# Column pairs of a split-precision decoder trunk: longer low weight parts, whole-row buffers, high-part products first

## The chip, the cores and the metric

The kernel runs on one core of one Trainium2 chip. The metric is device time in microseconds of one execution. Verdicts compare timed runs of two kernels on the same chip; the profile is one further execution, taken by the hardware profiler, and it has a time of its own.

## The reference

A trunk of two layers on 256 tokens of width 2048: a retention layer (8 heads, keys of 256, values of 512) with a squared-ReLU MLP, then a latent-attention layer (16 heads) with another such MLP. All inputs are float32.

```python
def sq_relu_mlp(h, w1, w2):
    return jnp.square(jax.nn.relu(h @ w1)) @ w2        # 2048 -> 8192 -> 2048

for layer in range(DEPTH):                              # DEPTH = 2
    if layer < N_A_LAYERS:
        h = rms_norm(x, norm_mix[layer])
        x = x + retention(h, ret_w_in[layer], ret_w_out[layer], ret_cos, ret_sin)
    else:
        ...
        h = rms_norm(x, norm_mix[layer])
        x = x + mla_attention(h, mla_w_dq[j], ..., mla_w_o[j], k_nope, k_pe, v, mla_cos, mla_sin)
    x = x + sq_relu_mlp(rms_norm(x, norm_mlp[layer]), mlp_w1[layer], mlp_w2[layer])
```

Nearly all of the work is in matrix products of the 256 tokens with weights that are read once from memory.

## The kernel before

**Two parts per number.** TensorE multiplies in the type fp32r. To keep float32 accuracy each operand is split in two: ScalarE rounds the value to fp32r (the high part, a copy, L188) and VectorE subtracts that from the value (the low part, L189). A product of two blocks is then three matmuls into one PSUM bank: activation high by weight high (L364), activation high by weight low (L365), activation low by weight high (L366). The activations are the stationary operand, 128 by 128, and the weights the moving one, 128 rows by 512 columns.

**Quads and pairs.** Most weights are laid out on the host in quads (`_quads`, L1110): 256 rows by 1024 columns, four blocks of 128 by 512, one load of 1 MB into a tile of 2048 columns. `gemm_pair` (L341) computes 1024 output columns (a column pair) as a loop over the quads of these columns, eight for 2048 rows, and adds into PSUM. A quad is multiplied with the 2 by 2 blocks of the activations (two groups of 128 tokens, two blocks of 128 rows) in one of two ways, chosen per quad by the tuple `kinds`: with eight products of blocks, or with seven, a scheme of the Strassen family. For seven, the quad needs sums of weight blocks: VectorE makes four of them in three instructions (L323, L327, L328: 1024, 512 and 512 columns) in two tiles `u` of 1024 columns, and the sums are split into parts as the blocks are. After the last quad `pair_out` (L376) copies the banks to SBUF (ScalarE) and combines them (VectorE).

**Parts of a quad.** `parts` (L302) splits up to 1024 columns at once into one buffer `wh` and one `wl` of 1024 columns each; there are five of either tag. A quad of eight makes two such pairs of parts; a quad of seven makes four: blocks b11 and b22, block b21 alone (512 columns), the sums u2 and u4, the sums u1 and u3. The products that use them are issued right after each, product by product.

**Other users of the same buffers.** `stream` (L210) feeds the plain products (`gemm`, `gemm_t`, `gemm_blocks`): it loads a chunk of up to 2048 columns and splits it in two halves, each into a `wh` and a `wl` of its own. Raw loads of either kind share three buffers (`raw`), and all are issued by SyncE's queue.

**What runs between quads.** Every quad and every chunk ends in a `tick`, which runs the functions that have become due: the evacuation of a finished pair, transposes of results into new activations, the chain of attention for a head. The order on each engine is then set by a scheduler, which moves instructions against each other where dependences allow; each engine executes its queue in that order, and an instruction that waits holds those behind it. `queued_behind` (L284) ties the low parts of blocks behind the last of the sums (`summed_up`, L328).

The stages in order are: retention (query and key products by `gemm_t`, gate and value products by pairs, output products by pairs), the first MLP (pairs `u` and `d`), the products of the latent attention (`kd`, `dqp`, `dq`, `ku`, `uq`, `wo`, `wop`), the second MLP. `kinds` comes from tuples at the top of the file: (1, 3, 5, 7), (3, 5, 7) and (5, 7) in the MLPs, (2, 4, 6, 7) and (5, 7) in retention, (3, 4, 6, 7) and (3, 5, 6, 7) in attention; the quads named have seven products.

## Time and profile before

| | |
|---|---|
| three timed runs | 2484.82, 2486.37, 2487.07 us |
| median | 2486.37 us |
| profiled execution | 2490.05 us |
| its span, first to last instruction | 2488.3 us |
| mean granted TensorE clock of it | 0.997 of full speed |
| read from memory | 479.14 MB |
| written | 39.85 MB |

The profile lists instructions by engine: PE is TensorE's matmuls, PEld its weight loads, DVE VectorE, ACT ScalarE, POOL GpSimd, SP SyncE. A group of instructions is named by its source line, its engine and its tiles, as out<-in; the numbers behind it are busy time, mean length, and the idle time of the engine just before it with what ended that. Names begin with the stage: `rp` gate and value pairs of retention, `ro` its output pairs, `u` and `d` the two products of an MLP. The end of a matmul is modelled, and matmuls overlap, so that spacing from start to start is the measure of TensorE's pace.

### The profile page before, as it was taken

To read this page: it belongs to the slowest core of one execution; us is meant where nothing else is said; L and a number is where in the kernel's file an instruction comes from. 1 tells how busy PE (TensorE), PEld (TensorE's weight loads), DVE (VectorE), ACT (ScalarE), POOL (GpSimd) and SP (SyncE) were. 2 spreads that over 40 slices of the span, in tenths; PEclk is the share of its full clock that TensorE was granted. 3 is DMA by queue.
4 is the path that set the end of the run, shared out by engine and by line. 5 is a ranking of instruction groups with operands and counts; after the bars stand their busy time and mean duration, and the time that the engine had idled before them with its cause. 6 is when DMAs were issued, how large, how long until landed. Compare 5 with 4: busy or idle time off the path is not lost.

```text
span 2488.3 us, 31679 instructions
## 1 busy us (share of the span) xinstructions
PE 2457.3 (99%) x11614; PEld 2066.6 (83%) x11614; DVE 2198.9 (88%) x2892; ACT 1648.2 (66%) x2297; POOL 251.4 (10%) x308
## 2 busy tenths in 40 slices
PE   9999999999999999999999999999999999999999
PEld 7788888888888888878888888998888888888887
DVE  6799999889899989989999988776899999999996
ACT  6566666566676767667676777666776667676663
POOL 7300001000010010010110101110000100100100
PEclk9999999999999999999999999999999999999999
DMA  9555558556565686685785554444555866857864
GB/s 312 190 190 204 177 193 256 207 174 223 200 216 191 207 252 200 213 260 187 238 269 203 192 206 174 155 146 170 174 207 207 236 224 200 260 202 223 260 212 167
DMA packets 93403, 521.04 MB, mean 209 GB/s; under 512 B 11072, under 2 KB 12224, under 8 KB 40000
## 3 DMA queue, kind: packets, MB, share of 16 engines
q1 hardware_dynamic: 71856, 472.83, 54.4%
q0 software_dynamic: 21248, 46.15, 8.8%
q8 instruction: 91, 1.49, 0.2%
q14 instruction: 64, 0.52, 0.1%
q10 hardware_dynamic: 144, 0.05, 0.0%
HBM read 479.14 MB, written 39.85 MB: 209 GB/s over the span
## 4 chain that ended last, share of the span: by engine, by line
PE 86%; DVE 7%; DMA 3%; ACT 2%; issue 1%; POOL 1%; DVEq 0%; ACTq 0%; POOLq 0%
PE u_c L365 6%; PE u_c L366 6%; PE u_c L364 6%; PE d_c L365 6%; PE d_c L366 6%; PE d_c L364 6%; PE rq_acc L276 2%; PE rp_c L364 2%; PE rp_c L365 2%; PE rp_c L366 2%; PE rk_acc L276 2%; PE u_p L364 2%; PE u_p L365 2%; PE u_p L366 2%; PE d_p L364 2%; PE d_p L366 2%
## 5 line engine op out<-in xcount | busy, mean ns | idle before, releaser
L189 DVE TENSOR_TENSOR d_wl<-d_raw,d_wh 128x1024 fp32r<-128x1024 f32 (+1 forms) x256 | 279.0, 1115 | 27.0 <-ACT d_wh L188 26.9
L188 ACT CAST d_wh<-d_raw 128x1024 fp32r<-128x1024 f32 (+1 forms) x256 | 241.9, 975 | 81.9 <-PE d_c L366 47.9
L189 DVE TENSOR_TENSOR u_wl<-u_raw,u_wh 128x1024 fp32r<-128x1024 f32 (+1 forms) x256 | 277.6, 1111 | 16.2 <-ACT u_wh L188 16.1
L188 ACT CAST u_wh<-u_raw 128x1024 fp32r<-128x1024 f32 (+1 forms) x256 | 240.9, 972 | 65.3 <-PE u_c L366 47.0
L365 PE MATMUL u_c<-u_wl,n 128*128 128x512 f32 x712 | 277.9, 390 | 2.8 <-DVE u_wl L189 2.8
L364 PE MATMUL u_c<-u_wh,n 128*128 128x512 f32 x712 | 278.4, 392 | 0.0
L366 PE MATMUL u_c<-u_wh,n 128*128 128x512 f32 x712 | 277.2, 389 | 0.0
L365 PE MATMUL d_c<-d_wl,hid 128*128 128x512 f32 x660 | 257.2, 390 | 3.0 <-DVE d_wl L189 3.0
L364 PE MATMUL d_c<-d_wh,hid 128*128 128x512 f32 x660 | 258.5, 392 | 0.0
L366 PE MATMUL d_c<-d_wh,hid 128*128 128x512 f32 x660 | 257.0, 389 | 0.0
L188 ACT CAST u_wh<-u_u 128x1024 fp32r<-128x1024 f32 x104 | 107.7, 1054 | 110.1 <-DVE u_u L328 55.7
L188 ACT CAST d_wh<-d_u 128x1024 fp32r<-128x1024 f32 x100 | 103.8, 1055 | 99.2 <-DVE d_u L328 55.1
L365 PEld LDWEIGHTS u_c<-u_wl,n 128*128 128x128 f32 x712 | 133.8, 188 | 32.3 <-DVE u_wl L189 5.2
L366 PEld LDWEIGHTS u_c<-u_wh,n 128*128 128x128 f32 x712 | 133.7, 188 | 27.7
L364 PEld LDWEIGHTS u_c<-u_wh,n 128*128 128x128 f32 x712 | 133.7, 188 | 27.2
L188 ACT CAST rp_wh<-rp_raw 128x1024 fp32r<-128x1024 f32 x112 | 104.1, 945 | 70.6 <-PE rp_c L366 42.3
L365 PEld LDWEIGHTS d_c<-d_wl,hid 128*128 128x128 f32 x660 | 124.0, 188 | 29.5 <-DVE d_wl L189 4.4
L366 PEld LDWEIGHTS d_c<-d_wh,hid 128*128 128x128 f32 x660 | 123.9, 188 | 25.8
L364 PEld LDWEIGHTS d_c<-d_wh,hid 128*128 128x128 f32 x660 | 124.0, 188 | 25.0
L189 DVE TENSOR_TENSOR u_wl<-u_u,u_wh 128x1024 fp32r<-128x1024 f32 x104 | 123.8, 1220 | 4.5 <-ACT u_wh L188 4.3
L189 DVE TENSOR_TENSOR rp_wl<-rp_raw,rp_wh 128x1024 fp32r<-128x1024 f32 x112 | 118.8, 1089 | 5.3 <-ACT rp_wh L188 5.0
L189 DVE TENSOR_TENSOR d_wl<-d_u,d_wh 128x1024 fp32r<-128x1024 f32 x100 | 118.8, 1219 | 2.6 <-ACT d_wh L188 2.6
(567 smaller groups left out, 6607.6 us busy)
## 6 DMA issues: line engine op xcount, KB each, us to landing
u_raw<-in_mlp_w SPq DMA_DIRECT2D x128, 1024.0 KB, 5.5
d_raw<-in_mlp_w SPq DMA_DIRECT2D x120, 1024.0 KB, 5.0
rp_raw<-in_ret_w_gv SPq DMA_DIRECT2D x56, 1024.0 KB, 4.9
ro_raw<-in_ret_w_out SPq DMA_DIRECT2D x32, 1024.0 KB, 5.1
uq_raw<-in_mla_w_uq SPq DMA_DIRECT2D x24, 768.0 KB, 4.2
rq_raw<-in_ret_w_qk SPq DMA_DIRECT2D x16, 1024.0 KB, 5.5
rk_raw<-in_ret_w_qk SPq DMA_DIRECT2D x16, 1024.0 KB, 4.9
xh<-d_c POOLq DMA_DIRECT2D x48, 256.0 KB, 6.2
```

Source lines behind the costliest of these rows:

```text
L188: nc.scalar.copy(h, src)
L189: return nc.vector.tensor_tensor(l, src, h.bitcast(F32), op=ALU.subtract)
L276: nc.tensor.matmul(acc[f], wh[:, cols], a.rearrange("p i s -> p (i s)"), start=k == 0, stop=k == nk - 1)
L364: nc.tensor.matmul(dst, ah, bh, start=n == 0, stop=False)
L365: nc.tensor.matmul(dst, ah, bl, start=False, stop=False)
L366: nc.tensor.matmul(dst, al, bh, start=False, stop=n == total[key] - 1)
```

## The change

The parts of a quad are made in whole rows. `parts` now takes one `wh` and one `wl` buffer of 2048 columns, fills the high buffer by the copies named in `highs` and the low one by the subtractions named in `lows`. A quad of eight has two copies of 1024 columns and one subtraction of 2048. A quad of seven has for its blocks b11, b22, b21 one copy and one subtraction of 1536 columns, and for its four sums two copies of 1024 and one subtraction of 2048. In the last quad of a pair (`whole`) the sums keep two subtractions of 1024 columns, u2 and u4 first.

There are three `wh` and two `wl` buffers of 2048 columns, where there were five and five of 1024; `stream` puts both halves of a chunk into one of each. The four sums of a quad stand in one tile of 2048 columns, one buffer, where there were two tiles of 1024 in two buffers. The host lays b21 ahead of b12, so that the three blocks stand side by side.

`mm` now gets all products of a quad at once. Where the quad is not the last of its pair, it issues for all products first the two matmuls with the high weight part, and then for all products the one with the low part; the products with the sums u1 and u3 come before those with u4 and u2. In the last quad it goes product by product, two high and one low, in the order of before.

```diff
     def stream(w, chunk, cols, name, use, done=None, before=None):
         raw = pool.tile([P, 2048], F32, tag="raw", bufs=3, name=f"{name}_raw")
+        high = pool.tile([P, 2048], F32R, tag="wh", bufs=3, name=f"{name}_wh")
+        low = pool.tile([P, 2048], F32R, tag="wl", bufs=2, name=f"{name}_wl")
...
         for half in range(2):
-            wh = pool.tile([P, 1024], F32R, tag="wh", bufs=5, name=f"{name}_wh{half}")
-            wl = pool.tile([P, 1024], F32R, tag="wl", bufs=5, name=f"{name}_wl{half}")
+            wh, wl = (v[:, half * n : (half + 1) * n] for v in (high, low))
...
-    def quad(w, chunk, x, mm, name):
+    def quad(w, chunk, x, mm, name, whole):
...
-        def parts(src, n, part, after=None):
-            wh = pool.tile([P, 1024], F32R, tag="wh", bufs=5, name=f"{name}_wh{part}")
-            wl = pool.tile([P, 1024], F32R, tag="wl", bufs=5, name=f"{name}_wl{part}")
-            low = low_part[0] = split(wh[:, : n * 512], wl[:, : n * 512], src)
-            if after is not None:
-                queued_behind(low, after)
-            return [[i[:, j * 512 : (j + 1) * 512] for i in (wh, wl)] for j in range(n)]
+        def parts(src, part, highs, lows, after=None):
+            high = pool.tile([P, 2048], F32R, tag="wh", bufs=3, name=f"{name}_wh{part}")
+            low = pool.tile([P, 2048], F32R, tag="wl", bufs=2, name=f"{name}_wl{part}")
+            for lo, hi in highs:
+                nc.scalar.copy(high[:, lo:hi], src[:, lo:hi])
+            for lo, hi in lows:
+                low_part[0] = nc.vector.tensor_tensor(
+                    low[:, lo:hi], src[:, lo:hi], high[:, lo:hi].bitcast(F32), op=ALU.subtract
+                )
+                if after is not None:
+                    queued_behind(low_part[0], after)
+            return [[i[:, j * 512 : (j + 1) * 512] for i in (high, low)] for j in range(4)]
 
         if more is None:
-            b11, b22 = parts(raw[:, 0:1024], 2, 0)
-            mm("c11", a(0, 0), b11)
...
-            b12, b21 = parts(raw[:, 1024:], 2, 1)
...
+            b11, b22, b21, b12 = parts(raw, 0, ((0, 1024), (1024, 2048)), ((0, 2048),))
+            mm([
+                ("c11", a(0, 0), b11),
...
+            ])
             return
-        u = [pool.tile([P, 2, 512], F32, tag="us", bufs=2, name=f"{name}_u{i}") for i in range(2)]
+        u = pool.tile([P, 2048], F32, tag="us", bufs=1, name=f"{name}_u")
...
-        b11, b22 = parts(raw[:, 0:1024], 2, 0, summed_up)
-        mm("p1", a(0, 0), b11)
-        mm("c12", s(3), b22)
-        (b21,) = parts(raw[:, 1536:], 1, 1, summed_up)
-        mm("c11", a(0, 1), b21)
-        u2, u4 = parts(u[1].rearrange("p i n -> p (i n)"), 2, 2)
-        mm("c21", a(1, 1), u4)
-        mm("p6", s(2), u2)
-        u1, u3 = parts(u[0].rearrange("p i n -> p (i n)"), 2, 3)
-        mm("p5", s(1), u1)
-        mm("p7", s(0), u3)
+        b11, b22, b21, _ = parts(raw, 0, ((0, 1536),), ((0, 1536),), summed_up)
+        lows = ((1024, 2048), (0, 1024)) if whole else ((0, 2048),)
+        u1, u3, u2, u4 = parts(u, 1, ((0, 1024), (1024, 2048)), lows)
+        ones, twos = [("c21", a(1, 1), u4), ("p6", s(2), u2)], [("p5", s(1), u1), ("p7", s(0), u3)]
+        mm([
+            ("p1", a(0, 0), b11),
+            ("c12", s(3), b22),
+            ("c11", a(0, 1), b21),
+            *(ones + twos if whole else twos + ones),
+        ])
...
-        def mm(key, lhs, rhs):
-            dst, n = get(key), count.get(key, 0)
-            count[key] = n + 1
-            (ah, al), (bh, bl) = lhs, rhs
-            nc.tensor.matmul(dst, ah, bh, start=n == 0, stop=False)
-            nc.tensor.matmul(dst, ah, bl, start=False, stop=False)
-            nc.tensor.matmul(dst, al, bh, start=False, stop=n == total[key] - 1)
+        def mm(products, whole):
+
+            def one(key, a, b):
+                n = count.get(key, 0)
+                count[key] = n + 1
+                nc.tensor.matmul(get(key), a, b, start=n == 0, stop=n == 3 * total[key] - 1)
+
+            for group in [[i] for i in products] if whole else [products]:
+                for key, (ah, al), (bh, bl) in group:
+                    one(key, ah, bh)
+                    one(key, al, bh)
+                for key, (ah, al), (bh, bl) in group:
+                    one(key, ah, bl)
...
-    w = np.stack([w[:, :, :, 0, 0], w[:, :, :, 1, 1], w[:, :, :, 0, 1], w[:, :, :, 1, 0]], axis=3)
+    w = np.stack([w[:, :, :, 0, 0], w[:, :, :, 1, 1], w[:, :, :, 1, 0], w[:, :, :, 0, 1]], axis=3)
```

The built program of the changed kernel differs beyond these lines, because the scheduler orders it anew. In a pair whose last two quads both have seven products it issues, in the last quad, eight high products and one matmul of the next stage ahead of the first low one.

More of the change, by code (lines that the diff above doesn't have):

```diff
@@ L310, in quad @@
-        if more is None:
-            b11, b22 = parts(raw[:, 0:1024], 2, 0)
-            mm("c11", a(0, 0), b11)
-            mm("c21", a(1, 0), b11)
-            mm("c12", a(0, 1), b22)
-            mm("c22", a(1, 1), b22)
-            b12, b21 = parts(raw[:, 1024:], 2, 1)
-            mm("c12", a(0, 0), b12)
-            mm("c22", a(1, 0), b12)
-            mm("c11", a(0, 1), b21)
-            mm("c21", a(1, 1), b21)
+        def parts(src, part, highs, lows, after=None):
[10 more added lines that the diff above has]
+            return [[i[:, j * 512 : (j + 1) * 512] for i in (high, low)] for j in range(4)]
@@ L321, in quad @@
+        if more is None:
+            b11, b22, b21, b12 = parts(raw, 0, ((0, 1024), (1024, 2048)), ((0, 2048),))
+            mm([
+                ("c11", a(0, 0), b11),
+                ("c21", a(1, 0), b11),
+                ("c12", a(0, 1), b22),
+                ("c22", a(1, 1), b22),
+                ("c12", a(0, 0), b12),
+                ("c22", a(1, 0), b12),
+                ("c11", a(0, 1), b21),
+                ("c21", a(1, 1), b21),
+            ])
             return
-        u = [pool.tile([P, 2, 512], F32, tag="us", bufs=2, name=f"{name}_u{i}") for i in range(2)]
+        u = pool.tile([P, 2048], F32, tag="us", bufs=1, name=f"{name}_u")
@@ L323, in quad @@
         nc.vector.tensor_tensor(
-            u[0], raw[:, 0:1024].rearrange("p (i n) -> p i n", i=2),
-            raw[:, 1024:1536].unsqueeze(1).to_broadcast([P, 2, 512]), op=ALU.add,
-        )
-        nc.vector.tensor_tensor(u[1][:, 0], u[0][:, 0], raw[:, 512:1024], op=ALU.add)
-        summed_up = nc.vector.tensor_tensor(u[1][:, 1], u[1][:, 0], raw[:, 1536:], op=ALU.add)
-        b11, b22 = parts(raw[:, 0:1024], 2, 0, summed_up)
-        mm("p1", a(0, 0), b11)
-        mm("c12", s(3), b22)
@@ L332, in quad @@
-        (b21,) = parts(raw[:, 1536:], 1, 1, summed_up)
-        mm("c11", a(0, 1), b21)
-        u2, u4 = parts(u[1].rearrange("p i n -> p (i n)"), 2, 2)
-        mm("c21", a(1, 1), u4)
-        mm("p6", s(2), u2)
-        u1, u3 = parts(u[0].rearrange("p i n -> p (i n)"), 2, 3)
-        mm("p5", s(1), u1)
-        mm("p7", s(0), u3)
+            u[:, 0:1024].rearrange("p (i n) -> p i n", i=2), raw[:, 0:1024].rearrange("p (i n) -> p i n", i=2),
+            raw[:, 1536:].unsqueeze(1).to_broadcast([P, 2, 512]), op=ALU.add,
+        )
@@ new lines, in quad @@
+        nc.vector.tensor_tensor(u[:, 1024:1536], u[:, 0:512], raw[:, 512:1024], op=ALU.add)
+        summed_up = nc.vector.tensor_tensor(u[:, 1536:], u[:, 1024:1536], raw[:, 1024:1536], op=ALU.add)
+        b11, b22, b21, _ = parts(raw, 0, ((0, 1536),), ((0, 1536),), summed_up)
+        lows = ((1024, 2048), (0, 1024)) if whole else ((0, 2048),)
+        u1, u3, u2, u4 = parts(u, 1, ((0, 1024), (1024, 2048)), lows)
+        ones, twos = [("c21", a(1, 1), u4), ("p6", s(2), u2)], [("p5", s(1), u1), ("p7", s(0), u3)]
@@ L341, in gemm_pair @@
+        mm([
+            ("p1", a(0, 0), b11),
+            ("c12", s(3), b22),
+            ("c11", a(0, 1), b21),
+            *(ones + twos if whole else twos + ones),
+        ])
     def gemm_pair(w, chunk0, act, kinds, name, done):
@@ L370, in gemm_pair @@
             v, more = act[i]
-            quad(w, chunk0 + i, (v, more if kinds[i] else None), mm, f"{name}{i}")
+            last = i == len(kinds) - 1
+            quad(w, chunk0 + i, (v, more if kinds[i] else None), lambda m, last=last: mm(m, last), f"{name}{i}", last)
             if i == len(kinds) - 1:
```

## Prediction

> **What bounds the kernel now.** I read the page's busy line first, then who TensorE waited for, then the timeline around one such wait.

> ```profile
> span 2488.3 us, 31679 instructions
> PE 2457.3 (99%) x11614; PEld 2066.6 (83%) x11614; DVE 2198.9 (88%) x2892; ACT 1648.2 (66%) x2297; POOL 251.4 (10%) x308
> ```

> TensorE leaves 2488.3 - 2457.3 = 31.0 us idle, and the change takes no matmul away, so nothing beyond those 31 us, and the short gaps that a modelled end covers, is to be had. The waits of TensorE, the longest first (total, times, longest):

> ```profile
> PE rg_acc L248 <- ACT a L190: 5.2, 1, 5.2
> PE qptp L207 <- ACT qt L1008: 3.3, 1, 3.3
> PE d_c L365 <- DVE d_wl L189: 3.0, 3, 1.3
> PE u_c L365 <- DVE u_wl L189: 2.8, 3, 1.4
> ...
> PE ro_c L365 <- DVE ro_wl L189: 1.6, 2, 1.3
> ...
> PE rp_c L365 <- DVE rp_wl L189: 0.8, 1, 0.8
> PE rp_p L365 <- DVE rp_wl L189: 0.7, 1, 0.7
> ```

> Only the rows of L365 lie in column pairs: the matmul with the low weight part, waiting for VectorE's subtraction. They are 3 + 3 + 2 + 1 + 1 = 10 waits and 3.0 + 2.8 + 1.6 + 0.8 + 0.7 = 8.9 us. What one really costs shows the timeline of TensorE. The first two rows below are the first matmuls of two quads that follow each other (the first of seven products, so 21 matmuls): 4.76 / 21 = 0.227 us from start to start. The last two are one wait:

> ```profile
> 429.52 0.39 PE L364 MATMUL rp_p<-rp_wh,a 128*128 128x512 f32 x1
> ...
> 434.28 0.39 PE L364 MATMUL rp_p<-rp_wh,a 128*128 128x512 f32 x1
> ...
> 1051.19 0.39 PE L364 MATMUL d_c<-d_wh,hid 128*128 128x512 f32 x1
> 1052.88 0.50 PE L365 MATMUL d_c<-d_wl,hid 128*128 128x512 f32 x1 [1.30 <-DVE d_wl L189]
> ```

> A matmul is drawn 0.39 long and the next may start after 0.227, so a wait costs 0.16 more than is shown: 1.69 - 0.227 = 1.46 here, and 8.9 + 10 x 0.16 = 10.5 us for the ten. Why VectorE was late there, in its timeline and in the chain of waits:

> ```profile
> 1039.88 1.22 DVE L189 TENSOR_TENSOR d_wl<-d_raw,d_wh 128x1024 fp32r<-128x1024 f32 x1
> 1041.01 0.69 DVE L327 TENSOR_TENSOR d_u<-d_u,d_raw 128x512 f32<-128x512 f32 x1
> 1041.73 0.69 DVE L328 TENSOR_TENSOR d_u<-d_u,d_raw 128x512 f32<-128x512 f32 x1
> 1042.34 1.82 DVE L189 TENSOR_TENSOR d_wl<-d_raw,d_wh 128x1024 fp32r<-128x1024 f32 x2
> 1044.08 2.35 DVE L189 TENSOR_TENSOR d_wl<-d_u,d_wh 128x1024 fp32r<-128x1024 f32 x2
> 1049.74 1.23 DVE L323 TENSOR_TENSOR d_u<-d_raw 128x1024 f32<-128x1024 f32 x1 [3.31 <-DMA d_raw<-in_mlp_w]
> 1051.00 0.69 DVE L327 TENSOR_TENSOR d_u<-d_u,d_raw 128x512 f32<-128x512 f32 x1
> 1051.61 2.35 DVE L189 TENSOR_TENSOR d_wl<-d_raw,d_wh 128x1024 fp32r<-128x1024 f32 x2
> ```

> ```profile
> 1041.12 8.52 DMA d_raw<-in_mlp_w
> ...
> 1052.84 0.04 issue
> 1052.88 0.50 PE d_c L365
> ```

> The low part that ends at 1041.1 frees a weight buffer, the load into it takes 8.52 us, the sums of that quad stand in VectorE's queue ahead of the low parts TensorE needs sooner, and TensorE waits.

> **The change part by part.** I call a quad S where it has seven products (21 matmuls, 4.76 us) and E where it has eight (24 x 0.227 = 5.45 us). There are 150 S and 202 E in 44 pairs.

> *Longer low parts.* The lengths, by form:

> ```profile
> L189 DVE TENSOR_TENSOR d_wl<-d_raw,d_wh 128x1024 fp32r<-128x1024 f32 x206 | 247.6, 1220 | 27.0 <-ACT d_wh L188 26.9
> L189 DVE TENSOR_TENSOR d_wl<-d_raw,d_wh 128x512 fp32r<-128x512 f32 x50 | 34.3, 685 | 0.0
> L323 DVE TENSOR_TENSOR d_u<-d_raw 128x1024 f32<-128x1024 f32 x50 | 61.0, 1221 | 19.2 <-DMA d_raw<-in_mlp_w 19.1
> ```

> 512 columns more cost 535 ns, so I take 1.755 us for 1536 and 2.29 for 2048 columns. The pairs in the timeline took 1.82 (1024 and 512) and 2.35 (twice 1024): an instruction saved is worth about 0.065 us, because neighbours overlap. An S loses two low parts (one in a pair's last quad, which keeps two halves), an E one: 106 x 2 + 44 + 202 = 458 instructions, 458 x 0.065 = 30 us of VectorE's 2199. Bounds: 0, where the overlap hides all of the fixed part, and 458 x 0.15 (1.220 - 2 x 0.535) = 69 us. None of it is TensorE time by itself; it moves the ten waits. The high copies lose 150 instructions of ScalarE, 66% busy; on the path they are worth nothing, and their cover is that idle third.

> [...]

> *High-part products first.* Before, the first low part of a quad was wanted one matmul after the quad's start. Now an E wants it after 16, 3.63 us, and an S after 14 (b) and 17 (u): 3.18 and 3.86 us. This is what I expect to pay off. The wait at 1052.88 again, with the built order (two sums of the coming S, then the low part of E): the b buffer of the S before is free 17 matmuls after that quad's start (1051.19 - 4.76 - 5.45 - 4.76 = 1036.2), at 1040.1, so the low part that frees the weight buffer runs 1040.2 to 1042.5, 1.4 later than before; load 8.52, landing 1051.0; sums 1.26 + 0.69; low part 2.29; ready 1055.3. TensorE wants it at 1051.19 + 3.63 = 1054.82: 0.5 lost in place of 1.46, a gain of 0.95. Over ten waits, of which the shorter vanish and the longest (1.4 + 0.16) leave 0.6, I count 1.5 us left of 10.5: **-9 us**. Bounds: -10.5, and +10, if the later release meets longer loads (second rival).

> *Two low buffers of a whole quad row, three high ones, one sum tile.* A low u part may now start only when the quad before has finished, and must be ready 3.86 us into its own: 3.86 - 0.10 - 2.29 = 1.47 us of play. The 0.10 is from the chain, matmul slot to VectorE:

> ```profile
> 1030.72 0.24 PE d_p L366
> ...
> 1031.06 0.70 DVE d_v L383
> ```

> Behind a waiting low part stand the sums of the next S, and behind them its high copies on ScalarE and its low parts. In the alternating pairs (E S E S) the walk closes: u part, 1.95 of sums, E part, last sum and b part take 8.9 of the 10.2 us. The evacuation of a finished pair (four sums, 2.6 us) falls into the next pair's first E, and the first u part is still ready 0.6 before it is wanted. I take 0 there; were that cover gone, each pair would pay the excess.

> Where two S close a pair (seven gate-value pairs, two output pairs of retention, the query pair and the output pair of attention: 11) the one sum tile bites: low u part 0.10 to 2.39 after the first S starts, only then the sums (1.26 + 0.73 + 0.61), then b: ready at 6.83. Product by product TensorE would want it at 4.76 + 0.45 = 5.21 and lose 1.6. The built program puts eight high products and one matmul of the next stage ahead: 4.76 + 9 x 0.227 = 6.80. Bounds per pair 0 and 1.6; near the first, 0.1: **+1 us**.

> *Streams.* The same half-width splits, with a lead of two chunks for low parts instead of two and a half. In the built order of the output projection ScalarE copies both halves of a chunk, no longer one, ahead of the last query's scaling, for which TensorE waits:

> ```profile
> 1709.52 1.03 ACT L188 CAST wo_wh<-wo_raw 128x1024 fp32r<-128x1024 f32 x1
> ...
> 1710.93 0.68 ACT L1008 ACTIVATE qt<-qntp,gqn 128x512 f32<-128x512 f32 x1
> ```

> ```profile
> 1711.67 1.11 PE L207 MATMUL qptp<-cst,qpp 128*128 128x128 f32 x4 [3.27 <-ACT qt L1008]
> ```

> One copy later is **+1 us**; bounds -3 (the wait goes) and +4, for the clock is low behind this wait and a longer one lengthens that too:

> ```profile
> 1712.00:1719.00 7.00, 7.00 (x34) 6.77 (x33) 2.95 (x6) 2.82 (x9) 0.00 (x0) 0.59 0.23 97
> ```

> (the eighth figure, 0.59, is the granted clock: 7 x 0.41 = 2.9 us).

> Sum: -9 + 1 + 1 = -7 us. The profiled execution took 2490.05 us, 3.7 above the median 2486.37 and 1.75 above its span; 2483 for such a run, **2479.4** for the median.

> **The rivals.** *All waits go:* the 30 us of VectorE give it enough lead that no low part comes late, the double S is filled, and some 2 us of gaps too short to be drawn go as well: -10.5 - 2 = -12.5, 2474. For it: 88% busy means lead is scarce now. Against: the wait at 1052.88 came from a load, not from VectorE's length. [...]

> *The loads decide, slower:*

> ```profile
> DVE u_u L323 <- DMA u_raw<-in_mlp_w: 23.1, 19, 3.1
> DVE d_u L323 <- DMA d_raw<-in_mlp_w: 19.1, 12, 3.3
> ```

> ```profile
> u_raw<-in_mlp_w SPq DMA_DIRECT2D x128, 1024.0 KB, 5.5
> d_raw<-in_mlp_w SPq DMA_DIRECT2D x120, 1024.0 KB, 5.0
> ```

> VectorE waited 31 times, 42.2 us, for a load, and its lead kept most of that from TensorE. With two low buffers the lead is 1.5 to 2.3 us, and an E releases its weight buffer up to 1.4 us later. From the point where loads ahead of an S take over 8.0 us (8.52 - 0.5) each microsecond is TensorE's. If half the 42.2 us comes through, 21 - 10.5 = +10.5, with the two +1 terms: 2499. Against: the median load is 5.5, and the later demand pays back what the later release takes.

> *The double S is not filled:* 11 x 1.6 = 17.6, less 9, plus 1: 2496. Against: it is in the built order.

> *It does not do what it says:* late loads are as late, the cushion is eaten by the later release, and the ten waits stay at 8 of 10.5 us: -2.5 + 2 = 2486.

> **How the numbers follow.** Forecast 0.42 (2475 to 2484), all waits gone 0.10, no effect 0.22, loads 0.20, double S 0.06. About 0.2%, 5 us, is what can be told from no change. Faster: 0.10 and most of 0.42, 0.46; same: the rest of the forecast and most of no effect, 0.27; slower: 0.27. The likeliest case alone is 2475 to 2484; the range that holds eight in ten reaches into both sides, 2471 to 2496.

> **What would show it.** Right: no wait of TensorE on a low part above 0.7 us, VectorE busy about 30 us less, 458 instructions fewer, single 2048-column parts of 2.29 us, the waits of VectorE for loads as long as now. Wrong: rows of TensorE waiting for the u low parts right after the 17th matmul (lead), or at the tenth matmul of a pair's last quad (double S); a 2048-column part well off 2.29; the wait for the last query's scaling changed by more than 3 us either way.

## The result and the profile after

The changed kernel took 2515.03 us (median of 4 runs, 2514.14 to 2518.75) beside 2486.72 for the kernel before on the same chip: ratio 1.0116, 95% interval 1.0095 to 1.0137, so about 28 us slower. The prediction said 2479.4 and a range of 2471 to 2496. The page of the changed kernel, its first lines (busy time, share of the span, instructions):

```profile
span 2513.4 us, 31023 instructions
PE 2469.2 (98%) x11614; PEld 2062.5 (82%) x11614; DVE 2164.8 (86%) x2434; ACT 1604.4 (64%) x2147; POOL 262.7 (10%) x308
```

VectorE has its 458 instructions less and is 34.1 us shorter (2198.9 before), and TensorE is the one that got worse. For whom it waited (total, times, longest):

```profile
PE hid_tp L207 <- ACT u_c L810: 13.6, 12, 4.0
PE rg_acc L249 <- ACT a L190: 5.3, 1, 5.3
PE qptp L207 <- ACT qt L1021: 3.7, 1, 3.7
PE n_tp L207 <- DVE x_mlp L486: 3.2, 2, 1.9
PE o L691 <- ACT vh L190: 2.6, 2, 1.5
PE kd_acc L250 <- DVE kd_wl L189: 2.2, 1, 2.2
```

The rows that named the low parts of the large pairs, 8.9 us before, are gone; of this kind only 0.3 us in the attention output pair is left. In their place stands a row that the kernel before does not have at all: the transposes of the hidden activations (`hid_tp`) wait for ScalarE's scaling of the pair's result (L810, the Relu, L797 before). The longest two of these are alike; one of them, in the chain of waits (start, length, what):

```profile
1282.60 2.30 DVE u_wl L309
1284.89 0.02 issue
1284.91 8.68 DMA u_raw<-in_mlp_w
...
1293.69 0.13 ACT u_wh L307
1293.82 1.25 issue
1295.06 0.73 ACT u_c L810
1295.79 0.04 issue
1295.84 1.54 PE hid_tp L207 x6
```

A low part ends at 1284.9 and frees a buffer for raw weights (`raw`); the load into it lands 8.68 us later; only then ScalarE makes the high copy of that quad, and only then the scalings, which have nothing to do with that load. Why, shows ScalarE's own timeline, first after, then before, at the same pair:

```profile
1286.17 0.76 ACT L810 ACTIVATE u_c<-u_c,n_r 128x512 f32<-128x512 f32 x1
1286.80 2.01 ACT L307 CAST u_wh<-u_raw 128x1024 fp32r<-128x1024 f32 x2
1293.69 1.47 ACT L307 CAST u_wh<-u_raw 128x1536 fp32r<-128x1536 f32 x1 [4.88 <-DMA u_raw<-in_mlp_w]
1295.06 1.94 ACT L810 ACTIVATE u_c<-u_c,n_r 128x512 f32<-128x512 f32 x3
```

```profile
1285.34 0.75 ACT L797 ACTIVATE u_c<-u_c,n_r 128x512 f32<-128x512 f32 x1
1285.96 2.96 ACT L188 CAST u_wh<-u_raw 128x1024 fp32r<-128x1024 f32 x3
1288.79 2.21 ACT L797 ACTIVATE u_c<-u_c,n_r 128x512 f32<-128x512 f32 x3
...
1292.89 1.57 ACT L188 CAST u_wh<-u_raw 128x1024 fp32r<-128x1024 f32 x2
```

Before, the last three scalings of a pair came ahead of the first high copy of the next pair's fourth quad (1292.89). After, that copy (1536 columns, the first quad of seven products) comes ahead of them, and it is the one that waits for a load. The rows of ScalarE show this order in all 16 up pairs of the changed kernel and in none of the kernel before. In 15 of the 16 the copy waits for its load, 31.4 us in all. VectorE's timeline of the changed kernel has the sums that the scalings need, with a low part among them; in the kernel before, one of half the length stood at that place (second view):

```profile
1286.34 2.29 DVE L309 TENSOR_TENSOR u_wl<-u_raw,u_wh 128x2048 fp32r<-128x2048 f32 x1
...
1291.68 0.68 DVE L410 TENSOR_TENSOR u_c<-u_c,u_p 128x512 f32<-128x512 f32 x1
```

```profile
1286.00 1.22 DVE L189 TENSOR_TENSOR u_wl<-u_raw,u_wh 128x1024 fp32r<-128x1024 f32 x1
...
1289.54 0.69 DVE L397 TENSOR_TENSOR u_c<-u_c,u_p 128x512 f32<-128x512 f32 x1
```

After the change the last sum was done at 1292.4, so from there to 1295.06 the queue, not the data, held the scalings.

To see every loss in one measure, also where no wait is drawn: for each width of matmul the median distance from one start to the next is the same in both kernels (0.227 us for 512 columns); what a matmul starts later than that is summed here by the tile that it writes, over all 11614 rows of TensorE. The kernels E are explained below.

```
us beyond median spacing       before  after    E1    E2    E8    E9   E10   E11   E12
u, d, ro (pairs, low parts)       9.8    6.7   4.6   2.6   2.8  -0.1  -0.5   5.3   0.9
hid (transposes)                  0.2   18.7   8.7   0.3  12.3   0.2   0.2   6.4   0.2
n, kd (next stage)                2.5    9.1   9.4   8.9   2.4   2.2   2.2   6.4   4.4
o (retention output)              0.4    3.1   3.0   2.9   0.4   0.3   0.3   0.7   0.4
wop, dqp (double S)               0.1    3.5   5.1   5.2   0.5   0.5   0.5   2.5   0.3
rp (double S)                     3.2    5.1   5.2   5.2   5.9   5.9   4.6   9.2   4.3
all others                       34.4   29.0  29.1  30.0  30.0  31.3  30.0  30.8  29.0
sum                              50.6   75.3  65.1  55.0  54.2  40.2  37.3  61.3  39.5
```

Of the 24.7 us between before and after, 18.5 lie at the transposes, 6.6 and 2.7 where a stage follows a pair, 5.3 in the double-S pairs; the first row gained 3.1. That row understates what the low parts gained. A matmul that runs while the granted clock is halved (0.50) counts where it writes, and 4.7 of the 6.7 us after the change are such matmuls, behind the waits of `hid_tp` (the windows in the last section show one place); without them 9.8 became 2.0. In E8 the whole 2.8 are of this kind, in the kernel before, E9 and E10 nothing. The 5.4 of "all others" are no gain of the change: every later kernel, those with the old buffers too, lies at 29 to 31 there, and 8.2 of the 34.4 before are matmuls under a halved clock, against 1.6 after.

### The profile page after: what moved, and what is told of

Read it like the earlier page. It is cut to its first block, busy times and chain, and to the rows that moved or that the text cites. A ratio compares the mean times of both kernels' runs of the same rounds, so it can differ in the third digit from the quotient of the medians.

```text
span 2513.4 us, 31023 instructions
## 1 busy us (share of the span) xinstructions
PE 2469.2 (98%) x11614; PEld 2062.5 (82%) x11614; DVE 2164.8 (86%) x2434; ACT 1604.4 (64%) x2147; POOL 262.7 (10%) x308
## 4 chain that ended last, share of the span: by engine, by line
PE 84%; DVE 6%; DMA 4%; ACT 3%; issue 2%; POOL 1%; SPq 0%; DVEq 0%; ACTq 0%; POOLq 0%
PE d_c L371 18%; PE u_c L371 18%; PE rp_c L371 7%; PE d_p L371 5%; PE ro_c L371 5%; PE u_p L371 5%; PE rp_p L371 3%; PE rk_acc L277 2%; PE rq_acc L277 2%; DMA u_raw<-in_mlp_w 2%; PE hid_tp L207 1%; PE ro_p L371 1%; PE rk_acc L273 1%; DVE u_wl L309 1%; PE wop_c L371 1%
## 5 line engine op out<-in xcount | busy, mean ns | idle before, releaser
L371 PE MATMUL u_c<-u_wh,n 128*128 128x512 f32 x1424 | 361.3, 395 | 0.2 <-ACT u_wh L307 0.2
L371 PE MATMUL d_c<-d_wh,hid 128*128 128x512 f32 x1320 | 331.3, 391 | 0.0
L371 PEld LDWEIGHTS u_c<-u_wh,n 128*128 128x128 f32 x1424 | 268.5, 190 | 55.6 <-ACT u_wh L307 0.6
L371 PEld LDWEIGHTS d_c<-d_wh,hid 128*128 128x128 f32 x1320 | 245.8, 188 | 49.8
L309 DVE TENSOR_TENSOR u_wl<-u_raw,u_wh 128x2048 fp32r<-128x2048 f32 (+1 forms) x128 | 264.5, 2068 | 0.9 <-PE u_c L371 0.4
L309 DVE TENSOR_TENSOR d_wl<-d_raw,d_wh 128x2048 fp32r<-128x2048 f32 x120 | 247.3, 2062 | 0.1
L371 PE MATMUL u_c<-u_wl,n 128*128 128x512 f32 x712 | 190.9, 389 | 0.0
L371 PE MATMUL d_c<-d_wl,hid 128*128 128x512 f32 x660 | 177.3, 389 | 0.0
L309 DVE TENSOR_TENSOR u_wl<-u_u,u_wh 128x2048 fp32r<-128x2048 f32 (+1 forms) x68 | 120.2, 1788 | 45.2 <-PE u_c L371 45.0
L371 PEld LDWEIGHTS u_c<-u_wl,n 128*128 128x128 f32 x712 | 133.8, 188 | 27.9
L309 DVE TENSOR_TENSOR d_wl<-d_u,d_wh 128x2048 fp32r<-128x2048 f32 (+1 forms) x65 | 115.6, 1797 | 43.0 <-PE d_c L371 40.7
L371 PEld LDWEIGHTS d_c<-d_wl,hid 128*128 128x128 f32 x660 | 123.9, 188 | 25.8
L371 PE MATMUL rp_c<-rp_wh,a 128*128 128x512 f32 x560 | 142.6, 391 | 1.3 <-DVE rk_u L647 0.8
L307 ACT CAST rp_wh<-rp_raw 128x1024 fp32r<-128x1024 f32 (+1 forms) x84 | 97.7, 1194 | 69.2 <-PE rp_c L371 37.0
L371 PEld LDWEIGHTS rp_c<-rp_wh,a 128*128 128x128 f32 x560 | 104.3, 188 | 24.2 <-issue 1.2
L309 DVE TENSOR_TENSOR rp_wl<-rp_raw,rp_wh 128x2048 fp32r<-128x2048 f32 (+1 forms) x56 | 112.6, 2017 | 0.0
## 6 DMA issues: line engine op xcount, KB each, us to landing
u_raw<-in_mlp_w SPq DMA_DIRECT2D x128, 1024.0 KB, 5.7
d_raw<-in_mlp_w SPq DMA_DIRECT2D x120, 1024.0 KB, 5.0
rp_raw<-in_ret_w_gv SPq DMA_DIRECT2D x56, 1024.0 KB, 4.9
ro_raw<-in_ret_w_out SPq DMA_DIRECT2D x32, 1024.0 KB, 4.9
rq_raw<-in_ret_w_qk SPq DMA_DIRECT2D x16, 1024.0 KB, 5.5
rk_raw<-in_ret_w_qk SPq DMA_DIRECT2D x16, 1024.0 KB, 4.8
```

The source lines that it names most:

```text
L307: nc.scalar.copy(high[:, lo:hi], src[:, lo:hi])
L309: low_part[0] = nc.vector.tensor_tensor(low[:, lo:hi], src[:, lo:hi], high[:, lo:hi].bitcast(F32), op=ALU.subtract)
L371: nc.tensor.matmul(get(key), a, b, start=n == 0, stop=n == 3 * total[key] - 1)
```

## The experiments

All ratios are to the kernel before, run on the same chip in the same session; its median there was 2482.5 to 2485.9.

**E1: the copy behind the scalings.** In the changed kernel, one order forced on ScalarE and nothing else:

```diff
-                nc.scalar.copy(high[:, lo:hi], src[:, lo:hi])
+                copied = nc.scalar.copy(high[:, lo:hi], src[:, lo:hi])
+                if after is not None and last_relu[0] is not None:
+                    queued_behind(copied, last_relu[0])
...
-                        nc.scalar.activation(c[t][i], c[t][i], AF.Relu, scale=r[t])
+                        last_relu[0] = nc.scalar.activation(c[t][i], c[t][i], AF.Relu, scale=r[t])
```

> The changed kernel with one order forced: the 1536-column high copies of seven-product quads stand on ScalarE behind the four scalings (Relu) of the pair before. Theory A (the copy, which waits for its load, holds up the scalings, for these TensorE waits before the transposes, and the clock halves behind the longest waits): TensorE's 13.6 us of waits for the scaling fall below 5, and the time falls from 2515 to 2497-2506. Rival B (the load itself is late, so the quad's own matmuls or low parts wait instead): waits move to rows of L371, time 2510-2516. Rival C (the scalings wait for VectorE's sums, which stand behind a 2048-column low part): waits for the scaling stay above 8 us, time 2508-2513.

2500.8 us, ratio 1.0065 (1.0051 to 1.0079), against 1.0116. TensorE's waits, the two rows that matter:

```profile
PE hid_tp L207 <- ACT u_c L812: 4.7, 5, 1.5
...
PE u_c L373 <- DVE u_wl L311: 1.3, 2, 0.7
```

13.6 became 4.7, and only 1.3 us came back at the low parts: theory A, not rival B. What is left at the same pair shows ScalarE's timeline:

```profile
1290.27 2.02 ACT L307 CAST u_wh<-u_raw 128x1024 fp32r<-128x1024 f32 x2
1294.06 0.72 ACT L812 ACTIVATE u_c<-u_c,n_r 128x512 f32<-128x512 f32 x1 [1.78 <-DVE u_c L412]
```

Now the scaling waits for VectorE's sums: rival C holds for the rest.

**E2: the sums ahead of the next low parts too.** As E1, and the same on VectorE: `last_sum` is the last instruction of `summed`, and each low part of a pair that is emitted after it gets `queued_behind(low_part[0], last_sum[0])`.

> As the run before, and the low parts of the quads that follow are put behind the finished pair's sums on VectorE as well. Theory A alone: no more than 2 us below the run before. Rival C (part of the wait is VectorE's order): 3 to 6 us below it, no wait of TensorE for a scaling above 0.5 us; 2492-2502. If the later low parts are then late, rows of L371 waiting for DVE appear and it is above the run before.

2494.88 us, ratio 1.0045 (1.0032 to 1.0058): some 5 us below E1 by the ratios, and no row of `hid_tp` is left (0.3 in the table, 0.2 before). The two queue orders together account for about 18 of the 29 us.

**E3: the reverse order in the kernel before.** Three of a pair's scalings are put behind the first high copy of the next pair's first seven-product quad.

```diff
         b11, b22 = parts(raw[:, 0:1024], 2, 0, summed_up)
+        for relu in relus[1:]:
+            queued_behind(relu, copied[0])
+        relus.clear()
```

> The kernel before with the reverse order forced: three scalings of a pair stand behind the first high copy of the next pair's first seven-product quad. Theory A: the loss appears in the old kernel: TensorE waits for the scaling 5 to 15 us in all, time 2493-2506. Rival B (the load is only late because of the new buffers): the scalings are not held up, 2485-2490.

2491.84 us, ratio 1.0039 (1.0026 to 1.0053): slower by 9 to 10 us, just under theory A's span. The waits of the profiled run are smaller than the 5 to 15 us expected:

```profile
PE hid_tp L207 <- ACT u_c L800: 2.2, 3, 1.4
```

So the loss can be made in the old kernel, but its size is only in part that of the change: of the 16 copies put ahead, three waited longer than 0.5 us for a load here (2.5 the longest), 15 in the changed kernel (5.3 the longest). The row explains part of the 9 us, as do the 4.7 us at the transposes by the measure of the table (0.2 before); the rest is not settled.

**E4: product by product in the changed kernel.** Every quad goes product by product, two high matmuls and one low, with buffers and lengths as changed. It is the old order but for the sums: outside a pair's last quad the products with u1 and u3 still come first.

```diff
-            quad(..., lambda m, last=last: mm(m, last), f"{name}{i}", last)
+            quad(..., lambda m: mm(m, True), f"{name}{i}", last)
```

> The changed kernel with the old order of matmuls in every quad (product by product), all buffers and instruction lengths as changed. If the high products first are what carries the low parts: TensorE waits for low parts of pairs 10 us or more in all, time 2520-2545. If the high products first are what makes the loads late (low parts done later, so raw buffers free later): the waits for the scaling go, time 2490-2510.

2533.9 us, ratio 1.0206 (1.0189 to 1.0223): in the range of the first theory, though hardly a wait for a pair's low part is drawn (2.1 us). The same measure as in the table gives 26.8 us for u, d and ro (6.7 in the change). The second expectation failed: the waits for the scaling did not go,

```profile
PE hid_tp L207 <- ACT u_c L810: 12.0, 7, 4.1
```

and ScalarE has the copy ahead of the scalings in all 16 pairs, as in the changed kernel. The loss at the low parts is made of small steps, one of which:

```profile
893.65 2.29 DVE L309 TENSOR_TENSOR d_wl<-d_u,d_wh 128x2048 fp32r<-128x2048 f32 x1 [1.73 <-PE d_c L371]
```

```profile
895.42 0.61 PE L371 MATMUL d_p<-d_wh,hid_more 128*128 128x512 f32 x2
896.00 0.50 PE L371 MATMUL d_p<-d_wl,hid_more 128*128 128x512 f32 x1
```

The low part of the sums could not start before its buffer was free (1.73 us of idle VectorE) and ends at 895.94; TensorE's matmul with it starts at 896.00, 0.35 us after the start of the last of the two before it (895.42 + 0.227), not 0.227. That the 26.8 us are steps of 0.1 us like this one is my reading of the window from 850 to 930 us: no idle time of TensorE is drawn there in either kernel, but it holds 348 matmuls in E4 and 355 in the change. With two low buffers of whole rows in both, the high products first made the difference of 26.8 to 6.7.

**E5: two high rows, three low rows.** As E2, `bufs=2` for the high and `bufs=3` for the low parts.

> As e2, with two high and three low buffers instead of three and two. If the lead of the low parts at the passage from a column pair to the next stage (both low buffers still held by the pair's last quad) is what is left of the loss: the wait for kd_wl of 2.2 us goes, the waits in the attention output pair shrink, time 3 to 8 us below e2, 2487-2492 beside a kernel before of 2483. If the high copies need their lead: waits of L371 for ACT appear, time 5 us or more above e2.

2526.84 us, ratio 1.0179 (1.0151 to 1.0207), 33 us above E2. The wait for `kd_wl`, 2.2 us in E2, is 2.8 here. The second expectation holds for the time; the first is not tested cleanly, since the high copies are now late too, as in this row of six waits that E2 does not have:

```profile
PE rk_acc L277 <- ACT rk_wh L188: 3.6, 6, 0.6
```

**E6: the values first.** As E2, and the high copies of the key weights (streams whose name begins with rk) behind the scaling that makes `vh`. The 1536-column copies of the seven-product quads that come after it are tied behind the same scaling, since they use the same variable.

> As e2, and the high copies of the key weights stand on ScalarE behind the value scalings of the retention head before. Theory (the same queueing as at the scalings of the multilayer part): the 2.4 us of waits o <- vh go, time 1 to 4 us below e2. Rival: the key copies are late in turn, rows of L273 or L277 wait, time as e2 or above.

2497.71 us, ratio 1.0057 (1.0037 to 1.0077), not to be told from E2. The waits for `vh` are gone, and another row has grown from 0.8 us to 3.4:

```profile
PE rp_c L378 <- DVE rk_u L654: 3.4, 6, 1.0
```

So one wait was exchanged for another. That the key copies, and not the quads' copies tied with them, made the new one was not tested apart.

**E7: short low parts in the changed kernel.** The lists of column ranges of `parts` cut to 1024 and 512 columns, all else as changed.

> The changed kernel with its low parts cut back to 512 and 1024 columns (each of 1536 into 1024 and 512, each of 2048 into two), all else as changed. If VectorE's time decides (its busy time rises by 50 us and more): slower than the change by 5 to 20 us, 2520-2535. If it doesn't, since the waits come from ScalarE's order and from buffers: 2511-2519, and VectorE's total is 20 to 35 us longer by the spacing of its instructions.

2517.66 us, ratio 1.0143 (1.0114 to 1.0173); the interval overlaps that of the change (1.0095 to 1.0137). VectorE's row:

```profile
PE 2465.2 (98%) x11614; PEld 2058.2 (82%) x11614; DVE 2194.2 (87%) x2892; ACT 1603.1 (64%) x2147; POOL 256.2 (10%) x308
```

2194.2 - 2164.8 = 29.4 us for 458 instructions, 0.064 us each. The pairs lose no more at their low parts than in the change (2.0 us for u, d and ro in the table's measure). The longer parts are not the loss; whether they are a small gain, as the distance of the two ratios would have it (0.0027, 7 us), the overlapping intervals do not settle.

**E8: the order of matmuls, in the kernel before.** Products are collected in a list and run at the end of the quad, the high ones first except in the pair's last quad; half-width buffers, five and five, short parts and the order of the products (u4 and u2 ahead of u1 and u3) stay. So the copies and subtractions of a quad are now all issued ahead of its first matmul, as they are in the changed kernel.

```diff
+            for group in [[i] for i in products] if whole else [list(products)]:
+                for key, (ah, al), (bh, bl) in group:
+                    one(key, ah, bh)
+                    one(key, al, bh)
+                for key, (ah, al), (bh, bl) in group:
+                    one(key, ah, bl)
```

> The kernel before, its five half-width buffers and short parts kept, with the high products of every quad but a pair's last one first. If the order alone gives what the change was worth in the pairs: TensorE's waits for low parts of pairs fall from 8.9 to below 3 us and the time to 2474-2481. If the order needs the whole-row buffers (a seven-product quad now holds four of the five until its end, so the next quad's parts start late): 2495-2540, waits of L-rows of the pairs for DVE or ACT above 10 us.

2493.32 us, ratio 1.0036 (1.002 to 1.0052): neither expectation. The low parts are as hoped (9.8 to 2.8 us in the table), and yet the kernel is slower, by the row that the changed kernel has too:

```profile
PE hid_tp L207 <- ACT u_c L808: 10.6, 5, 3.3
```

In all 16 pairs the high copy of the fourth quad stands ahead of the last three scalings, as after the change. So neither whole-row buffers nor longer parts are needed for the new order on ScalarE. The high products first are not needed either: E4, product by product, has it too. What E4, E8 and the change share is that all parts of a quad are issued before its matmuls; that this is the cause was not tested alone.

**E9 and E10: that order, with the queues put right.** E9 is E8 with the high copies of seven-product quads behind the scalings (as E1, where it is the 1536-column copy alone), E10 has the sums ahead of the low parts as well (as E2).

> As e8 (half-width buffers and short parts of before, high products first), with the high copies of seven-product quads behind the pair's scalings on ScalarE. If the order of matmuls is worth its part and only the copies' place on ScalarE ate it: the 10.6 us of waits for the scaling fall below 3, time 9 to 13 us below e8, that is 2 us above to 6 us below the kernel before. If the loads decide: e8's time, 2490 or more beside a kernel before of 2483.

> As e9, and the pairs' sums ahead of the next low parts on VectorE, as in e2: the same to 3 us below e9. It differs from e2 by buffers, lengths and streams alone; if these are what is left of the loss, it lies 10 to 18 us below e2, and the waits kd_acc, n_tp, o and wop_p that e2 has are as in the kernel before.

E9: 2478.46 us, ratio 0.9984 (0.9975 to 0.9992). E10: 2478.6 us, ratio 0.9982 (0.9971 to 0.9993). Both are faster than the kernel before, by about 4 us, and so than either kernel. No row of `hid_tp` remains.

E10 lies 0.63% or 15.6 us below E2, which has the same two queue orders: that is the price of the rest of the change (whole-row buffers, one sum tile, longer parts, shared buffers in the streams, the products with u1 and u3 first) once the queues are right. In the table it is n and kd 6.7, wop and dqp 4.7, the pairs 3.1, o 2.6.

**E11 and E12: how many halves.** E10 with six half-width buffers for high parts and four for low ones, as many bytes as the change has (E11), and with four and six (E12), where E10 has five and five.

> As e10 with the change's amounts of buffer in half-width pieces: six halves for the high parts and four for the low parts, for five and five. If the amount of low buffer is what costs at the passages between stages (two whole rows are four halves): waits for kd_wl and in the wop pair as in e2, time 3 to 10 us above e10. If it is that a whole row is taken and given back at once: within 2 us of e10.

> As e10 with four halves for the high parts and six for the low parts, the other side of e11. If low buffers are scarce on their own account: 2 to 6 us below e10, 2472-2477 beside a kernel before of 2482.5. If five and five is the balance (a seven-product quad takes four high halves, so with four nothing of the next quad is copied before the first of them is free): 5 us or more above e10, waits for ACT copies in the pairs.

E11: 2501.58 us, ratio 1.0077 (1.0061 to 1.0093), 23 us above E10 where 3 to 10 were expected. E12: 2480.39 us, ratio 0.9979 (0.9967 to 0.9991), the same as E10, so neither of its expectations held. Two rows of E11:

```profile
PE hid_tp L207 <- ACT u_c L812: 4.3, 9, 0.6
...
PE kd_acc L249 <- DVE kd_wl L189: 3.0, 4, 1.7
```

The fifth low half is worth 23 us here, even against a sixth high one; a sixth low half in place of a high one gains nothing. The 24.0 us between E10 and E11 in the table are spread: 6.2 at the transposes, 5.8 in the pairs, 4.6 in rp, 4.2 at n and kd. The wait for `kd_wl`, 1.1 us in E10 and 2.2 after the change, is back without any whole-row buffer; but E12 has 2.2 us of it too, with six low halves and four high ones, so it does not follow the low buffers alone. And four high halves (E12) cost nothing, while two whole high rows, as many bytes, cost 33 us in E5. That speaks for the grain and against the amount; the two kernels differ in more than that.

## Why the prediction was wrong, point by point

**Late low parts, -9: right in the mechanism.** In E10 the pairs' excess falls from 9.8 to -0.5 us, by 10.3; in E2, with whole rows, by 7.2; in the change itself by 7.8, when the matmuls under the halved clock are left out. In time E10 gains only 4 us of its 10.3; 1.4 went to rp, and the rest is not accounted for. No wait of TensorE on a pair's low part passes 0.3 us in the changed kernel. That this comes from the order of matmuls and not from the longer parts show E8 and E7.

**Longer low parts, 30 us of VectorE: right, and no gain in time shown.** Lengths by form, after the change:

```profile
L309 DVE TENSOR_TENSOR u_wl<-u_raw,u_wh 128x2048 fp32r<-128x2048 f32 x76 | 173.4, 2284 | 0.5
...
L309 DVE TENSOR_TENSOR u_wl<-u_raw,u_wh 128x1536 fp32r<-128x1536 f32 x52 | 91.0, 1751 | 0.4 <-PE u_c L371 0.4
```

2.284 and 1.751 us, forecast 2.29 and 1.755; 0.064 us saved an instruction (E7), forecast 0.065.

**"On the path they are worth nothing, and their cover is that idle third": this step failed.** It priced the high copies of ScalarE by the engine's share of busy time. A third of idle time covers work that may run at any time; it does not cover a place in a queue. The copy that was moved waits for a load (4.88 us at 1293.69 above), and what stands behind it waits too (the scalings from 1295.06, whose sums were done at 1292.4). ScalarE's waits of the changed kernel say so in two rows, which were 1.4 and 1.7 us in the kernel before:

```profile
ACT u_wh L307 <- DMA u_raw<-in_mlp_w: 46.8, 26, 5.3
...
ACT d_wh L307 <- DMA d_raw<-in_mlp_w: 29.2, 22, 2.1
```

The prediction expected VectorE's waits for loads to stay as long as they were. They went to ScalarE instead (VectorE's rows for u and d, 42.2 us before, are 4.8 and 1.8 now), and 31.4 us of ScalarE's stand right in front of the scalings. The built order, which the prediction used for the double S and for the last query's scaling, has the copy's new place in it; the prediction did not follow the scalings there. Undone alone, this order gives back 13 us by the ratios of E1 (1.0116 to 1.0065) and 13 from E8 to E9.

**The finished pair's evacuation, "I take 0 there": failed too.** I walked it on VectorE until the next u part and found 0.6 us to spare, but did not ask when the sums that TensorE's transposes need are done. Where a low part of 1024 columns stood among them (1286.00 above), one of 2048 stands now (1286.34), and the last sum is done at 1292.4, where it was 1290.2. E2, which puts no low part among the sums, lies about 5 us below E1; that is what the order costs.

**Streams, +1 with bounds of -3 and +4: mis-sized.** The place that I priced, the last query's scaling, came out at +0.4 (3.3 to 3.7 us). The low clock behind it, which I expected to last longer with a longer wait, lasted 3.41 us where it was 6.83 before: the two profiles do not show that a longer wait lengthens it. The lead of the low parts, which I named beside it without pricing, looks like the larger matter. The passage into the down projections, VectorE after the change and then before:

```profile
1418.59 2.35 DVE L309 TENSOR_TENSOR d_wl<-d_u,d_wh 128x1024 fp32r<-128x1024 f32 x2
1420.86 1.88 DVE L486 TENSOR_TENSOR x_mlp<-d_c,x_mlp 128x512 f32<-128x512 f32 x3
...
1428.91 0.81 DVE L189 TENSOR_TENSOR kd_wl<-kd_raw,kd_wh 128x640 fp32r<-128x640 f32 x1
```

```profile
1411.35 0.82 DVE L189 TENSOR_TENSOR kd_wl<-kd_raw,kd_wh 128x640 fp32r<-128x640 f32 x1
1412.47 0.69 DVE L473 TENSOR_TENSOR x_mlp<-d_c,x_mlp 128x512 f32<-128x512 f32 x1 [0.31 <-ACT d_c L381]
1413.10 0.83 DVE L189 TENSOR_TENSOR kd_wl<-kd_raw,kd_wh 128x640 fp32r<-128x640 f32 x1
```

Before, the first low parts of `kd` came between the last residual additions and gave TensorE matmuls to fill with; after, the first comes behind all of them, 8 us after the pair's last low part. At n and kd this cost 6.6 us; another 2.7 lie at o, where TensorE waits for a scaling on ScalarE (`vh`). E11, with four halves for low parts and six for high ones, brings n and kd to 6.4 us, E12, with six and four, to 4.4, where E10 with five and five has 2.2; how E2's 15.6 us divide between streams, double S and buffers was not tried.

**Double S, 11 x 0.1 = +1: low.** rp, wop and dqp rose by 5.3 us over nine pairs (7, 1 and 1); the two pairs of ro are in the table's first row. The mean of 0.6 lies inside the bounds of 0 and 1.6, but hides a spread. In rp it is 1.9 us, 0.3 a pair, and the kernels with two sum tiles have about as much (E8 and E9 5.9, E10 4.6, the change 5.1), so the one tile is not shown to be the cause there. The wop pair alone rose by 2.4 us, above the bound, dqp by 1.0. In the wop pair a high copy was waited for (0.9 us), and the prediction had priced sums and low parts alone.

**The rival with late loads** gave 2499 by another road: lead lost on VectorE. The late load did decide at the longest waits, but through ScalarE's queue, and its price, 18.5 us at the transposes, was above the 10.5 that this rival added.

## What to carry to other kernels

When a change makes a scheduler order anew, compare the listing on every engine for instructions that wait on a load, and ask what stands behind them; an engine's idle share was no cover for that here (ScalarE was 66% busy before, and 31.4 us of its waits came ahead of the scalings). Price the number of buffers in every stage that uses them, at the passages between stages too and not only in the steady loop: four low halves for five cost 23 us, spread over four places. A part of a losing change may be a gain: here the order of matmuls, with the queue orders pinned, beats the kernel it came from by about 4 us.

## What the hardware showed that was not expected

```profile
1287.00:1292.00 5.00, 5.00 (x24) 3.78 (x22) 4.97 (x7) 1.81 (x2) 0.00 (x0) 1.00 0.98 393
...
1296.00:1300.00 4.00, 4.00 (x13) 3.42 (x14) 1.96 (x3) 3.04 (x6) 0.00 (x0) 0.50 0.65 244
1300.00:1303.00 3.00, 3.00 (x11) 2.35 (x11) 2.42 (x6) 1.05 (x1) 0.00 (x0) 0.75 0.03 14
1303.00:1310.00 7.00, 7.00 (x37) 5.88 (x36) 4.47 (x8) 5.55 (x9) 2.13 (x4) 1.00 0.45 139
```

4 x 0.5 + 3 x 0.25 = 2.75 us, an estimate from these rows, on top of a wait of 3.83. But length alone did not decide: in E2 a wait of 1.87 us at 443 was followed by half clock, and in the changed kernel one of 2.08 at 1470 by none:

```profile
445.20:449.00 3.80, 3.58 (x11) 3.00 (x12) 3.60 (x4) 1.73 (x3) 0.00 (x0) 0.56 0.61 248
```

```profile
1472.60:1477.00 4.40, 4.33 (x22) 3.55 (x23) 3.31 (x7) 3.15 (x7) 0.00 (x0) 1.00 0.29 76
```

The profile's clock records of the changed kernel have the halved clock (0.50) begin at 1294.66, 1427.78, 1724.74, 2038.76 and 2380.10 us, whole multiples of 3.413 us apart (39, 87, 92 and 100 of them), and last one or two such steps (3.41 us twice, 6.83 three times). E2's 1.87 us of waiting ended at 445.42, and by its row above the half clock began at about 445.6 (an estimate: 3.8 x 0.44 / 0.5 = 3.3 us of half clock up to 449), so the whole wait lay in the step before that. If the steps of the changed kernel are carried on from 1427.78, thirteen of them end at 1472.15, and its 2.08 us of waiting were split there into 1.57 and 0.5. How much idle time in a step was enough these runs do not settle. In the kernel before, with the steps carried on from 1635.77 in the same way, 1.88 us of idle TensorE in the step from 1632.4 were followed by half clock (0.50 for 6.83 us); 1.75 in the step from 1454.9 and 1.90 in that from 2482.3, after the last matmul, were not (1.00 in the next step).
